# Ending the third and fourth spans of an opening's work order one row earlier

## The chip, the cores and the metric

One Trainium2 chip, one of its cores. The metric is the device time of one execution in microseconds (us), the median over runs of the same program. The engines are named as in the profile: PE is TensorE's matmul, PEld its weight load, DVE is VectorE, ACT is ScalarE, POOL is GpSimd, SP is SyncE, which here does nothing but issue DMAs.

## The reference

A trunk of two layers over 256 tokens of 2048 features. Each layer is a token mixer followed by a gated feed-forward network; ahead of each of these stands an RMS norm with a scale and a shift that are computed from a conditioning vector `c`. Layer 0 mixes with retention over 8 heads, layer 1 with a short convolution. The change lies in the beginning of layer 0:

```python
c_act = silu(c)
mod = c_act @ w_mod[i] + b_mod[i]                  # w_mod[i]: 2048 x 12288
sh1, sc1, g1, sh2, sc2, g2 = split(mod, 6)
h = rms_norm(x, norm1_g[i]) * (1 + sc1) + sh1      # 256 x 2048
q, k, v, g = split(h @ ret_w_in, ...)              # 2048 x (2048 + 2048 + 4096 + 4096)
q, k = rope(q), rope(k) * 256 ** -0.5              # 8 heads of 256
o = rms_norm(retention(q, k, v))                   # decaying causal attention, 8 heads
x = x + g1 * ((silu(g) * o) @ ret_w_out)
```

All arrays are float32.

## The kernel before, in words

Tokens lie in the free dimension. The 2048 features of `h` are 16 blocks of 128 partitions, called rows 0 to 15 (`h[k]`). A product of one row with one block of 128 output columns is a unit; its weights are a 128x128 block (64 KB). Each float32 operand is split in a high part (`hi`, rounded to the type fp32r) and a low rest (`lo`), and a product is three fast matmuls, hi*hi, hi*lo and lo*hi, into one PSUM bank half. The weights stand in memory in the order of use (`w_all`), cut into chunks of 128x2048, that is 16 units or 1 MB. A chunk is fetched by SP into one of four `raw` buffers, and `prepare` splits half of it (a piece, 8 units) at a time: a cast on ACT (line 426, `hi`), then a subtraction on DVE (line 429, `lo`). There are five places for split pieces, and two pieces are kept ready ahead of the one in use.

Before a row can be used, its scale and shift must be known, and these are products of `c` with 1 MB of `w_mod` each. The weights of row k are loaded by `loaded` (two DMAs), reduced on DVE against the activated `c` (`reduced`, line 805, one for SC1, one for SH1), turned into two columns on ACT (line 814), and applied to the normed `x` (ACT lines 832 and 833, DVE line 834, which writes the row's low part). Line 823 norms the `x` of two rows (`norm_two`). So every row costs 2 MB of DMA and two long DVE instructions, and while the rows come in one by one, PE is given products that need only the rows that exist. This opening is a written-out order in five spans, `SPANS`, each a pair of heads (or one) with a range of rows. All partial sums of a span, q (two column blocks), k (two) and g (four) of each head, are held open in PSUM: eight banks for a pair of heads, four for one head. Within a row the head's two q blocks go to its first bank, the two k blocks to its second, the 512 columns of g to its third and fourth, one for each half of the tokens; then comes the second head.

At the end of a span its banks are emptied by `held`: the first time for a head by an ACT copy to SBUF (line 792), the second time by a DVE addition to that copy (line 789). Of a span's eight additions, four are issued at once and four are put in the list of due work:

```python
for i, pt in enumerate(span(g, plain_rows if g is RET_SPANS[1] else ())):
    key = (heads[i // 4], i % 4)
    if key not in ahead or i < 4:
        held(key, pt)
    else:
        due.append((step[0] + 0.2 * (i - 4), lambda key=key, pt=pt: held(key, pt)))
```

The order on DVE and ACT is as issued here. `more` is called at the start and in the middle of each row of a span. It issues all work of the list `due` whose time has come, and then moves the clock `step` on; a row of a pair of heads is one step (16 units), a row of one head half a step. Row k is due (`row_due`) 1.4 steps after the one before for the first two, 1.8 for the next two, 2.2 for the others: row 8 at step 10.8, row 9 at 13.0, row 10 at 15.2, row 11 at 17.4, row 15 at 26.2. One third of the way to the next row stands the reduction SC1 of that next row, two thirds of the way `after_scale` with its reduction SH1 and, every other row, `norm_two`. If a span needs a row that hasn't been issued, `more` issues all of the list up to that row at once, whatever its time. `row_due` also asks SP for the `w_mod` of the row after next.

After the spans come the heads in the order 4, 0, 2, 1, 5, 3, 6, 7. For each, q, k and g are finished over the rows that the spans left out (`pair`; these are the usual products), v is computed over all rows, and scores and outputs follow. The q and k blocks of heads 1 and 3 go through `product` (lines 479 and 482: one matmul of 512 and one of 256 columns for a unit), all others through `packed` (three of 256 columns, lines 541 to 543, or for 512-wide weights three of 512 columns for each half of the tokens, lines 492 to 494). From the end of the spans, reductions of later modulations (line 333) are mixed in by `paced`, 28 of them between unit `early` and unit 1024, where `early` is the number of units in the spans.

Of the kernel before, what the change touches and what calls it, by code (L numbers as in the profile page):

```python
# [30 lines left out]

CHUNK = 2048
HALF = 1024
SPANS = (((0, 1), (0, 2)), ((2, 3), (0, 5)), ((0, 1), (2, 10)), ((2, 3), (5, 13)), ((4,), (0, 16)))
HEAD_ORDER = (4, 0, 2, 1, 5, 3, 6, 7)
ROW_STEPS, ROWS_AT, PREPARED = (1.4, 1.8, 2.2), (4, 6), 1.0
ON_SCALAR, ON_VECTOR, SUMMED = ((0, 1, -1, 2, 3, -2, 4, 6, -3, -4), ((0, 1), (2, 3), 5, (4, 5), 7, (6, 7)), (1, 3, 5, 7))
# [42 lines left out]
def ret_in_groups():  # L80

    qkg, v = [], []
    for h in range(HEADS):
        q = [Q0 + h * DK + i * P for i in range(2)]
        k = [K0 + h * DK + i * P for i in range(2)]
        qkg.append([q, k, [(G0 + h * DV, DV)]])
        v.append(Group([V0 + h * DV], DV))  # L90
    done = [0] * HEADS
    spans = []
    for heads, (a, b) in SPANS:
        assert all(done[h] == a for h in heads)
        for h in heads:
            done[h] = b
        spans.append(Group([c for h in heads for part in qkg[h] for c in part], ks=range(a, b)))
    rest = [[Group(c, ks=range(done[h], KT)) for c in qkg[h]] for h in range(HEADS)]
    return spans, list(zip(rest, v))
# [6 lines left out]
def out_groups(parts, tail, lead):  # L106

    cols = [c * P for c in range(KT)]
    out = []
    for ks in parts:  # L110
        led = cols[:lead]
        out.append([Group(led, ks=ks[:-tail])] + [Group([c], ks=ks[-tail:]) for c in led])
        out[-1] += [Group([c], ks=ks) for c in cols[lead:]]
    return out


def head_rows():

    n = DV // P
    ks = [n * h + i for h in HEAD_ORDER for i in range(n)]  # L120
    return [ks[: len(ks) // 2], ks[len(ks) // 2 :]]
# [6 lines left out]
RET_SPANS, RET_HEADS = ret_in_groups()  # L128
FIRST_KS = SPANS[0][1][1]
RET_OUT = out_groups(head_rows(), DV // P, LEAD_RET)  # L130
# [135 lines left out]
def trunk(ctx: ExitStack, tc: tile.TileContext, x_in, c_in, pos_in, w_mod, cols_in, gain_in, tab_in, w_all, out):  # L266
# [462 lines left out]
    with ExitStack() as inner:  # L729
# [64 lines left out]
        with tc.tile_pool(name="start", bufs=1) as sp:  # L794
# [196 lines left out]
            def span(g, plain=()):  # L991
                n = g.n // 2
                return packed(
                    g, h, before=lambda k: more(n, k), between=lambda k: more(n), banks=[bank() for _ in range(n)],
                    plain=plain,
                )

            with tc.manual_schedule(engines={mybir.EngineType.DVE, mybir.EngineType.Activation}):
                for (heads, _), g in zip(SPANS[1:-1], RET_SPANS[1:-1]):
                    for i, pt in enumerate(span(g, plain_rows if g is RET_SPANS[1] else ())):  # L1000
# [576 lines left out]
```

## Time and profile before

| | |
|---|---|
| median of 3 runs | 2555.41 us (2555.26 to 2556.01) |
| the profiled execution | 2555.34 us, of it 2553.6 us in the profile's span |
| PE busy | 2539.3 us (99%) |
| PEld busy | 2184.0 us (86%) |
| DVE busy | 2352.9 us (92%) |
| ACT busy | 1352.8 us (53%) |
| DMA | 689.49 MB, mean 270 GB/s |
| granted TensorE clock | 0.998 of full speed |

The page gives each engine's busy time; matmuls are pipelined, and the duration given for one is longer than the distance to the next, so the distance between starts is what a matmul costs in a stream. In a timeline a line has the start in us from the span's beginning, the duration, the engine, the line of the program, the operation with output<-input, a count of merged instructions, and, where the engine was idle before, for how long and what ended it. A table by windows has for each stretch its length, then the busy time and number of instructions (x) for PE, PEld, DVE, ACT and POOL, then the granted clock, the DMA engines' share and the GB/s moved.

### The profile page before, as it was taken

The page shows a single profiled execution, that of the slowest core. Times are in us where ns is not written, and L with a number is a line of the kernel's source. Part 1 is how long each engine was busy: PE and PEld are TensorE (multiplying, and loading weights), DVE is VectorE, ACT ScalarE, POOL GpSimd, SP SyncE. Part 2 cuts the span into 40 slices and gives each one's busy share as a digit, 9 for nine tenths or more (in the row PEclk, how much of TensorE's full clock was granted, in tenths as well). Part 3 has the DMA queues.
Part 4 walks back from the last instruction along what each step waited for, and adds up shares of the span by engine and source line. Part 5 has one row for each costly group of instructions (what it writes and reads, how often), then busy time and mean ns, then how long its engine had stood idle before and what let it go on. Part 6 is the DMA issues. An engine that isn't in the chain of part 4 may idle for free.

```text
span 2553.6 us, 34841 instructions
## 1 busy us (share of the span) xinstructions
PE 2539.3 (99%) x13281; PEld 2184.0 (86%) x13281; DVE 2352.9 (92%) x2967; ACT 1352.8 (53%) x1800; POOL 182.4 (7%) x234
## 2 busy tenths in 40 slices
PE   9999999999999999999999999999999999999998
PEld 7898888888889888888888898888998888888887
DVE  7989999898899999889999899888989999999998
ACT  5544543454456554345555454445566555555555
POOL 0000121011110001000000012000000000000001
PEclk9999999999999999999999999999999999999999
DMA  9977888879875667866568879888845565565653
GB/s 398 414 314 270 314 319 339 333 286 334 324 281 214 237 232 297 338 246 231 214 231 302 324 275 338 321 305 308 322 159 215 180 229 216 181 215 182 230 183 148
DMA packets 96698, 689.49 MB, mean 270 GB/s; under 512 B 10745, under 2 KB 12169, under 8 KB 13457
## 3 DMA queue, kind: packets, MB, share of 16 engines
q1 hardware_dynamic: 96528, 687.25, 72.3%
q8 instruction: 104, 1.70, 0.3%
q14 instruction: 66, 0.53, 0.1%
HBM read 685.11 MB, written 2.11 MB: 269 GB/s over the span
## 4 chain that ended last, share of the span: by engine, by line
PE 93%; DVE 4%; DMA 1%; issue 1%; ACT 0%; POOL 0%; ACTq 0%; POOLq 0%; SPq 0%; DVEq 0%
PE bank L479 22%; PE bank L492 17%; PE bank L493 17%; PE bank L494 17%; PE bank L482 11%; DVE lo L429 2%; PE bank L543 1%; PE bank L542 1%; PE bank L541 1%; PE bank L674 1%; PE bank L676 1%; PE bank L675 1%; PE bank L1304 1%; PE bank L1081 1%; DMA raw<-w_mod 1%; DMA raw<-w_all 1%
## 5 line engine op out<-in xcount | busy, mean ns | idle before, releaser
L426 ACT CAST hi<-raw 128x1024 fp32r<-128x1024 f32 (+1 forms) x984 | 992.0, 1019 | 952.6 <-PE bank L494 337.0
L429 DVE TENSOR_TENSOR lo<-raw,hi 128x1024 fp32r<-128x1024 f32 (+1 forms) x984 | 1142.3, 1178 | 123.7 <-ACT hi L426 113.5
L492 PE MATMUL bank<-hi,h 128*128 128x512 f32 x1540 | 602.2, 391 | 0.0
L493 PE MATMUL bank<-lo,h 128*128 128x512 f32 x1540 | 600.8, 390 | 0.0
L494 PE MATMUL bank<-hi,h 128*128 128x512 f32 x1540 | 600.1, 390 | 0.0
L333 DVE SCALAR_TENSOR_TENSOR raw<-raw,cb 128x2048 f32<-128x2048 f32 x160 | 365.5, 2286 | 9.2 <-DMA raw<-w_mod 8.9
L479 PE MATMUL bank<-h,hi 128*128 128x512 f32 x1012 | 352.7, 392 | 0.0
L494 PEld LDWEIGHTS bank<-hi,h 128*128 128x128 f32 x1540 | 289.3, 188 | 60.8
L492 PEld LDWEIGHTS bank<-hi,h 128*128 128x128 f32 x1540 | 289.4, 188 | 57.9
L493 PEld LDWEIGHTS bank<-lo,h 128*128 128x128 f32 x1540 | 289.5, 188 | 57.3 <-DVE lo L429 0.4
L479 PE MATMUL bank<-mid,hi 128*128 128x512 f32 x920 | 319.4, 391 | 0.0
L482 PE MATMUL bank<-h,lo 128*128 128x256 f32 x1012 | 284.8, 281 | 0.0
L482 PE MATMUL bank<-mid,lo 128*128 128x256 f32 x920 | 259.5, 282 | 0.0
L479 PEld LDWEIGHTS bank<-h,hi 128*128 128x128 f32 x1012 | 190.0, 188 | 40.4
L479 PEld LDWEIGHTS bank<-mid,hi 128*128 128x128 f32 x920 | 172.7, 188 | 35.8
L482 PEld LDWEIGHTS bank<-h,lo 128*128 128x128 f32 x1012 | 191.5, 189 | 0.5
L482 PEld LDWEIGHTS bank<-mid,lo 128*128 128x128 f32 x920 | 174.2, 189 | 0.1
L479 PE MATMUL bank<-rm,hi 128*128 128x512 f32 x496 | 172.5, 391 | 0.0
L482 PE MATMUL bank<-rm,lo 128*128 128x256 f32 x496 | 139.9, 282 | 0.0
L492 PE MATMUL bank<-hi,mid 128*128 128x512 f32 x284 | 110.7, 390 | 0.0
L494 PE MATMUL bank<-hi,mid 128*128 128x512 f32 x284 | 110.6, 389 | 0.0
L493 PE MATMUL bank<-lo,mid 128*128 128x512 f32 x284 | 110.6, 389 | 0.0
(301 smaller groups left out, 3352.7 us busy)
## 6 DMA issues: line engine op xcount, KB each, us to landing
raw<-w_all SPq DMA_DIRECT2D x456, 1024.0 KB, 4.9
raw<-w_mod SPq DMA_DIRECT2D x192, 1024.0 KB, 6.0
x<-x_in SPq DMA_DIRECT2D x4, 512.0 KB, 5.6
out<-xt SPq DMA_DIRECT2D x4, 512.0 KB, 2.7
decay<-tab_in SPq DMA_DIRECT2D x8, 128.0 KB, 5.4
x<-gate_row SPq DMA_DIRECT2D x2, 512.0 KB, 4.7
last_gain<-gain_in SPq DMA_DIRECT2D x1, 1024.0 KB
cols<-cols_in SPq DMA_DIRECT2D x1, 152.0 KB, 8.4
```

The source lines that it names most:

```text
L333: nc.vector.scalar_tensor_tensor(raw, raw, 1.0, cb, op0=ALU.mult, op1=ALU.mult, accum_out=total)
L426: nc.scalar.copy(hi[:, o], raw[:, o])
L429: nc.vector.tensor_tensor(lo, raw, hi.bitcast(F32), op=ALU.subtract)
L479: nc.tensor.matmul(pt, hi, h, start=fresh and k == g.ks[0], stop=False, skip_group_check=True)
L482: nc.tensor.matmul(pt[:, 1, :], lo, h[:, 0, :], start=False, stop=last and k == g.ks[-1], skip_group_check=True)
L492: nc.tensor.matmul(o, hi, w_hi, start=first, stop=False)
L493: nc.tensor.matmul(o, hi, w_lo, start=False, stop=False)
L494: nc.tensor.matmul(o, lo, w_hi, start=False, stop=last)
L541: nc.tensor.matmul(pt, hi, h[:, 0, :], start=first, stop=False, skip_group_check=True)
L542: nc.tensor.matmul(pt, hi, h[:, 1, :], start=False, stop=False, skip_group_check=True)
L543: nc.tensor.matmul(pt, lo, h[:, 0, :], start=False, stop=last, skip_group_check=True)
L674: nc.tensor.matmul(pt, hi, high, start=k == 0, stop=False, skip_group_check=True)
```

## The change

The third span (heads 0 and 1) ends with row 8 in place of row 9, and the fourth (heads 2 and 3) with row 11 in place of row 12. Row 9 of heads 0 and 1 and row 12 of heads 2 and 3, 16 units each, are computed with the heads' remaining rows after the opening. The layout of the weights follows, and so does `early`, which falls from 496 units to 464. Nothing else is edited.

```diff
-SPANS = (((0, 1), (0, 2)), ((2, 3), (0, 5)), ((0, 1), (2, 10)), ((2, 3), (5, 13)), ((4,), (0, 16)))
+SPANS = (((0, 1), (0, 2)), ((2, 3), (0, 5)), ((0, 1), (2, 9)), ((2, 3), (5, 12)), ((4,), (0, 16)))
```

## The prediction

> **What bounds the kernel now.** I read the page's first lines first, then its chain that ended last, then the list of what PE waited for.
>
> ```profile
> span 2553.6 us, 34841 instructions
> PE 2539.3 (99%) x13281; PEld 2184.0 (86%) x13281; DVE 2352.9 (92%) x2967; ACT 1352.8 (53%) x1800; POOL 182.4 (7%) x234
> PE 93%; DVE 4%; DMA 1%; issue 1%; ACT 0%; POOL 0%; ACTq 0%; POOLq 0%; SPq 0%; DVEq 0%
> PE bank L543 <- DVE lo L429: 1.8, 3, 0.9
> PE bank L542 <- DVE h L834: 0.3, 1, 0.3
> PE bank L1081 <- DVE sp L559: 0.5, 1, 0.5
> ```
>
> PE carries the end: 93% of the chain is its own. The last three lines are waits of PE in the first 250 us (us in total, times, longest); the first of them lies ahead of the changed place and is touched by nothing here. From 108 us to the end of the span the list has one entry, the 0.5 us on `sp`. So every us by which PE stalls in the opening is a us of the total, and there is hardly a wait left behind the opening that could be won back.
>
> The opening itself has two other engines near their limit, as the table by windows shows.
>
> ```profile
> 4.00:8.00 4.00, 2.77 (x12) 1.91 (x12) 0.77 (x3) 2.71 (x6) 0.00 (x0) 0.92 0.97 373
> 8.00:12.00 4.00, 4.00 (x15) 3.34 (x15) 3.27 (x5) 2.62 (x5) 0.00 (x0) 0.66 1.04 424
> 64.00:68.00 4.00, 3.13 (x20) 2.67 (x19) 4.00 (x6) 3.72 (x9) 0.00 (x0) 1.00 1.01 422
> 96.00:120.00 24.00, 23.71 (x150) 21.19 (x149) 23.54 (x28) 10.64 (x14) 0.00 (x0) 1.00 1.01 420
> 168.00:192.00 24.00, 24.00 (x158) 21.95 (x157) 18.38 (x19) 12.43 (x17) 0.00 (x0) 1.00 0.73 272
> ```
>
> From 96 to 120 us DVE is busy 23.54 of 24 us and the DMA engines all of the time; by 168 us both have slack. The changed boundary falls in the tight stretch. PE's timeline there:
>
> ```profile
> 99.61 0.28 PE L541 MATMUL bank<-h,hi 128*128 128x256 f32 x1
> 101.04 0.40 PE L492 MATMUL bank<-hi,h 128*128 128x512 f32 x1
> 101.74 0.40 PE L492 MATMUL bank<-hi,h 128*128 128x512 f32 x1
> 102.20 0.39 PE L494 MATMUL bank<-hi,h 128*128 128x512 f32 x1
> 102.43 0.28 PE L541 MATMUL bank<-h,hi 128*128 128x256 f32 x1
> 105.25 0.31 PE L541 MATMUL bank<-h,hi 128*128 128x256 f32 x1
> 105.85 0.39 PE L542 MATMUL bank<-h,hi 128*128 128x256 f32 x1 [0.29 <-DVE h L834]
> 108.66 0.28 PE L541 MATMUL bank<-h,hi 128*128 128x256 f32 x1
> 111.47 0.28 PE L541 MATMUL bank<-h,hi 128*128 128x256 f32 x1
> ```
>
> Row 8 of the third span runs from 99.61 to 105.25 us, one head from 99.61 to 102.43. Half a row costs 2.82 us, a row 5.64. Within the half, the g matmuls begin 1.43 us after its start (101.04), those for the second half of the tokens 0.70 later (101.74). Row 9 starts at 105.25, and its first half takes 108.66 - 105.25 = 3.41 us in place of 2.82: PE loses 0.59 us for the low part of row 9, forced at step 12 ahead of its due time 13.0.
>
> **The change part by part.** First, the row that PE waits for. The third span no longer uses row 9; its first use moves to the fourth span, step 16, three steps behind its due time. Gone: **-0.59 us**. Late next is not another row but what takes its place, the emptying of the banks. Both spans need all eight, so the fourth span's first row can't write a bank before the third's sum has been added from it (`held`). Before, this came after the rush for row 9, and DVE did it so:
>
> ```profile
> 97.50 0.42 DVE L834 TENSOR_TENSOR h<-u,h 128x256 fp32r<-128x256 f32 x1
> 99.21 2.28 DVE L805 SCALAR_TENSOR_TENSOR raw<-raw,cb 128x2048 f32<-128x2048 f32 x1
> 101.42 2.29 DVE L805 SCALAR_TENSOR_TENSOR raw<-raw,cb 128x2048 f32<-128x2048 f32 x1
> 103.64 0.69 DVE L823 TENSOR_TENSOR two<-x,rb 128x512 f32<-128x512 f32 x1
> 104.24 1.22 DVE L429 TENSOR_TENSOR lo<-raw,hi 128x1024 fp32r<-128x1024 f32 x1
> 105.38 0.42 DVE L834 TENSOR_TENSOR h<-u,h 128x256 fp32r<-128x256 f32 x1
> 107.25 3.07 DVE L789 TENSOR_TENSOR rm<-rm,bank 128x512 f32<-128x512 f32 x5
> 110.23 1.22 DVE L429 TENSOR_TENSOR lo<-raw,hi 128x1024 fp32r<-128x1024 f32 x1
> 111.37 1.28 DVE L789 TENSOR_TENSOR rm<-rm,bank 128x512 f32<-128x512 f32 x2
> 113.70 0.68 DVE L789 TENSOR_TENSOR rm<-rm,bank 128x512 f32<-128x512 f32 x1
> 114.30 2.29 DVE L805 SCALAR_TENSOR_TENSOR raw<-raw,cb 128x2048 f32<-128x2048 f32 x1
> ```
>
> One sees row 8's low part (97.50), the two reductions for row 9 and a norm (99.21 to 104.24), row 9's low part (105.38), and then eight additions as 5, 2 and 1 among splits, with no reduction until 114.30. The seventh ended by 112.6, and its bank, the second head's first g bank, was wanted at 114.3 + 1.43 = 115.7: hidden, by 3 us. From start to start, an addition costs (110.23 - 107.25)/5 = 0.60 us, a split 111.37 - 110.23 = 1.14, a reduction 101.42 - 99.21 = 2.21, the norm 104.24 - 103.64 = 0.60.
>
> After, the span's end is at step 12, while the reductions of row 9 keep their times, 11.53 (SC1) and 12.27 (SH1, with the norm); `more` issues only at whole and half steps, so they come out at 12.0 and 12.5. The deferred additions are due at 12.0, 12.2, 12.4 and 12.6. Sorted, the order on DVE becomes: additions 0 to 3, SC1, addition 4, split, addition 5, SH1, norm, addition 6, split, addition 7, split, row 9's low part. Two reductions and the norm now stand among the additions. Up to 99.21 us both programs are the same. The fourth addition waits for its bank's last matmul, 102.20 + 0.39 = 102.59. From there: addition to 103.19, SC1 to 105.40, addition 4 to 106.00, split 107.14, addition 5 to 107.74, SH1 109.95, norm 110.55, addition 6 ends 0.68 after that start, 111.23; the split begins at 111.15 and gives way at 112.29, addition 7 ends at 112.97.
>
> PE starts the fourth span at 105.25 and wants the second head's first g bank at 105.25 + 2.82 + 1.43 = 109.50. It gets it at 111.23: 1.73 us lost. The second bank is wanted 0.70 later, at 111.93, and is free at 112.97: 1.04 more. **+2.77 us**. The banks of both heads' q and k and of the first head's g are free in time (addition 5 at 107.74 against 108.07 + 0.71). The split weights for the next row are ready by 112.29. Bounds for this term: nothing at the low end, as before, where the same additions hid; at the high end 2.77 plus one more reduction ahead of addition 7, 2.21, so 4.98. I take the worked value, since every duration in it is a row.
>
> Queued behind these on DVE: the split for the row after next (wanted near 119) and row 9's low part, now near 114.4 us, wanted at step 16, past 128 us. SP is held up too: `w_mod` of row 11, two issues behind row 9, and a chunk of `w_all` wait until those `raw` buffers are read, near 110 to 112 us. They are used 12 us and more later, so I cost them nothing; DMA will show a gap instead.
>
> The second boundary, span four to five, comes at step 19 with the reductions of row 12 at the same places, but the fifth span takes four banks, and the four immediate additions free these: nothing. The fifth span starts two steps sooner, so rows 13 to 15 are wanted 11.3 us earlier against their due times. Row 15 is the tight one:
>
> ```profile
> 184.79 0.28 PE L541 MATMUL bank<-h,hi 128*128 128x256 f32 x1
> 184.80 0.42 DVE L834 TENSOR_TENSOR h<-u,h 128x256 fp32r<-128x256 f32 x1 [0.31 <-ACT h L833]
> 187.62 0.28 PE L541 MATMUL bank<-h,hi 128*128 128x256 f32 x1
> ```
>
> It is issued in the middle of the row that starts at step 26, and its low part ended at 185.22, 0.43 us after that row's start (184.79). After, the very next row, 2.83 us on, is row 15: a margin of 2.4 us, where DVE is busy 18.38 of 24. Nothing.
>
> The moved units: 32 in all, of which the q and k units of heads 1 and 3, 2 x 4, change from three 256-column matmuls to one of 512 and one of 256.
>
> ```profile
> 306.31 0.39 PE L479 MATMUL bank<-h,hi 128*128 128x512 f32 x1
> 306.66 0.40 PE L479 MATMUL bank<-h,hi 128*128 128x512 f32 x1
> ```
>
> Such a unit takes 306.66 - 306.31 = 0.35 us; in the opening four take 1.43, so 0.357. Eight units: -0.06 us. The other 24 run the same matmuls. Their weight splits (four pieces, 4.6 us of DVE) and two `w_all` chunks of 1 MB move with them, behind PE. `paced` keeps its 28 reductions, each with its DMA and its small POOL operations, over 560 units in place of 528: thinner, no cost. With them moves the 0.5 us wait on `sp`: it may go, or double.
>
> Sum: 2555.34 - 0.59 + 2.77 - 0.06 = 2557.46. The profiled execution stands 0.07 under the median of 2555.41, so I forecast 2557.5 us, 0.08% slower. A measurement here tells about 0.2%, 5.1 us, from no change; this is inside it.
>
> **The rivals.** *The additions stay hidden* and only the wait for row 9 goes: 2555.41 - 0.65 = 2554.8. It needs additions 6 and 7 ahead of SH1, or a DVE that runs 3.5 us earlier. For it: before, all eight hid. Against: DVE's order follows the list, and DVE has no slack there.
>
> *PE's clock falls in the stall.* In the windows, 4 to 8 us has PE busy 2.77 of 4 us and the clock at 0.92, then 0.66: a loss of (0.08 + 0.34) x 4 = 1.7 us. 64 to 68 has 3.13 busy at 1.00. The predicted stall leaves PE busy some 2.3 us in one stretch of 4, nearer to the first. That gives 2557.5 + 1.7 = 2559.2. [...]
>
> *Slower by over 0.2%: row 15 comes late.* Place: the last row of the fifth span. It decides once its low part comes more than 2.4 us later against PE than before; from there each us is a us. To pass 2560.5 takes 2.4 + 3.0 = 5.4 us. For it: 11 us of lead are given up. Against: DVE's slack there, and the same work at the same steps. At 6 us late the time is 2561.1.
>
> *Faster by over 0.2%* has no place: PE's waits from the boundary on are 0.59 and 0.5.
>
> **How the numbers follow.** Forecast 0.60; additions hidden 0.20; clock 0.12; row 15 late, or another stall of that size, 0.06; faster 0.02. The range goes from the hidden case less 0.2 of scatter, 2554.6, to the clock case with the `sp` wait doubled and some of the upper bound, 2560.0. The forecast's own range is 2556.9 to 2558.3. Within 0.2% lie the first three, 0.92.
>
> **What would show it.** In the changed trace PE has no wait for `h` at 105 us, but two waits on DVE's line 789 in the first row of the fourth span, near 111 and 113 us, of about 1.7 and 1.0 us, and line 805 stands between additions. The clock stays at 1.00. The DMA share dips after 105 us. No wait is seen at row 15. It is wrong if PE waits on something else there, if line 789 shows no wait, or if the heads' part grows.

## The result, and the profile after

The changed kernel takes 2564.67 us (median of 5 runs, 2563.68 to 2566.73) against 2555.66 us before: ratio 1.0036, interval 1.0025 to 1.0046, 9.0 us slower. The span of its profiled execution is 9.2 us longer. The page's first lines, the one group of PE on the page that now has idle time before it, and PE's waits from 80 to 250 us (total, times, longest; behind 250 us there are none):

```profile
span 2562.8 us, 34842 instructions
PE 2543.1 (99%) x13273; PEld 2185.2 (85%) x13273; DVE 2356.0 (92%) x2967; ACT 1354.7 (53%) x1800; POOL 182.5 (7%) x234
L492 PE MATMUL bank<-hi,h 128*128 128x512 f32 x1540 | 601.8, 391 | 2.4 <-DVE rm L789 2.4
PE bank L1054 <- ACT k L1025: 2.4, 1, 2.4
PE bank L492 <- DVE rm L789: 2.4, 2, 1.7
PE bank L1081 <- ACT sp L558: 1.4, 1, 1.4
PE bank L1057 <- DVE k L1026: 0.6, 1, 0.6
```

The work is the same; the waits are not. Two are the forecast ones on the additions (line 789). The others are for `k` and `sp` of head 4, the first head behind the opening. PE's timeline gives what each place costs:

```profile
108.47 0.28 PE L541 MATMUL bank<-h,hi 128*128 128x256 f32 x1
114.26 0.28 PE L541 MATMUL bank<-h,hi 128*128 128x256 f32 x1
190.41 0.28 PE L541 MATMUL bank<-h,hi 128*128 128x256 f32 x1
217.57 0.57 PE L1054 MATMUL bank<-q,k 128*128 128x512 f32 x1 [2.43 <-ACT k L1025]
226.81 0.96 PE L1081 MATMUL bank<-v,sp 128*128 128x512 f32 x3 [1.38 <-ACT sp L558]
231.84 0.28 PE L541 MATMUL bank<-h,hi 128*128 128x256 f32 x1
```

The fourth span's first row: its second half takes 114.26 - 108.47 = 5.79 us in place of 2.82, **+2.97**; row 9's 0.59 is saved. Row 15 starts at 190.41, and the matmuls behind head 4's second output group at 231.84: 41.43 us. Before, the same two points were at 198.90 and 233.54:

```profile
198.90 0.28 PE L541 MATMUL bank<-h,hi 128*128 128x256 f32 x1
233.54 0.28 PE L541 MATMUL bank<-h,hi 128*128 128x256 f32 x1
```

That is 34.64 us, so **+6.79**. The sum, 2.97 - 0.59 + 6.79 = 9.17, accounts for the 9.2 us (this execution came to the place 0.4 us later than the one before, and about as much is made up behind head 4). Of the 6.79, 2.4 and 0.6 are waits for k (its high part, then its low part) and 1.4 one for sp, less the 0.5 us on sp that was there before. Nearly all of the rest, 2.9 us, is in the clock. By windows (length, busy time and count of PE, PEld, DVE, ACT, POOL, then granted clock, DMA share, GB/s):

```profile
216.00:217.00 1.00, 0.00 (x0) 0.00 (x0) 1.00 (x4) 0.81 (x2) 0.00 (x0) 1.00 0.90 377
218.00:219.00 1.00, 0.42 (x2) 0.28 (x2) 1.00 (x3) 0.00 (x0) 0.00 (x0) 0.50 0.90 377
222.00:223.00 1.00, 1.00 (x7) 1.00 (x6) 1.00 (x3) 0.00 (x0) 0.00 (x0) 0.50 0.00 0
224.00:225.00 1.00, 1.00 (x7) 1.00 (x7) 1.00 (x1) 0.00 (x0) 0.00 (x0) 0.65 0.76 131
```

After the wait PE ran at half its clock from about 218 to 224.7 us, from 218.72 on through matmuls without a gap.

### The profile page after: what moved, and what is told of

Its sections match the earlier page's. It is cut to its first block, busy times and chain, and to the rows that moved or that the text cites. A ratio compares the mean times of both kernels' runs of the same rounds, so it can differ in the third digit from the quotient of the medians.

```text
span 2562.8 us, 34842 instructions
## 1 busy us (share of the span) xinstructions
PE 2543.1 (99%) x13273; PEld 2185.2 (85%) x13273; DVE 2356.0 (92%) x2967; ACT 1354.7 (53%) x1800; POOL 182.5 (7%) x234
## 4 chain that ended last, share of the span: by engine, by line
PE 94%; DVE 3%; DMA 1%; issue 1%; ACT 0%; POOL 0%; ACTq 0%; POOLq 0%; DVEq 0%; SPq 0%
PE bank L479 22%; PE bank L492 17%; PE bank L493 17%; PE bank L494 17%; PE bank L482 11%; DVE lo L429 1%; PE bank L543 1%; PE bank L541 1%; PE bank L542 1%; PE bank L674 1%; PE bank L676 1%; PE bank L675 1%; DMA raw<-w_all 1%; PE bank L1304 1%; PE bank L1081 1%
```

## The experiments

Each is an edit of the changed kernel, unless it says otherwise; differences are between medians of runs on the same chip.

**held_at_once**

```diff
-                        if key not in ahead or i < 4:
+                        if True:
```

> The changed kernel with all eight additions of a span issued at its end, none deferred, so that no reduction stands between them. What the changed trace has to be explained: the boundary costs 2.97 us there (half a row that takes 5.79 us in place of 2.82), head 4's scores and what follows cost another 6.8 us, and 0.59 us is saved on row 9; sum 9.2 us. Theory 'two places': the boundary and the scores are separate, so this run loses the 2.97 us and keeps the rest, about +6.2 us on the kernel before; the order on DVE after the opening is the same as in the changed kernel, so the wait for k at head 4's scores stays about 2.4 us. Rival 'one place': the stall at the boundary shifts DVE and PE against each other and causes the late k; then both go, and the time is 0.6 us under the kernel before. [...]

Measured: 2561.84 us, +5.9 on the kernel before (ratio 1.0023, 1.0013 to 1.0032). PE's wait on line 789 is gone, and the waits at head 4 are there to the tenth:

```profile
PE bank L1054 <- ACT k L1025: 2.4, 1, 2.4
PE bank L1081 <- ACT sp L558: 1.4, 1, 1.4
```

So there are two places, and the first costs what its row says.

**angles_early**

```diff
-                due.append((at + (i + 1) * 0.5, turn))
+                due.append((at - 5.0 + (i + 1) * 0.5, turn))
```

> The changed kernel with the six steps of the rope's angles due 5 steps sooner, within the fifth span, so that they no longer stand behind row 15's low part. Theory 'chain': k of head 4 is late (2.4 us wait, then 0.6 for its low part, then a clock of 0.50 for 7 us, then 1.4 on sp) because angles, rope of q and rope of k start only when row 15 is done, and in the changed kernel row 15 is done half a row before the spans' end. Then these waits go and what is left is the boundary: -0.59 + 2.97, and less the 0.5 us wait on sp that the kernel before had: +1.9 to +2.4 us on the kernel before, no clock under 1.00 after 200 us. Rival 'reductions': the reductions of later modulations, which begin 32 units sooner, push k; then the wait shrinks little and the time stays near +9 us. Rival 'row 15': row 15 itself is late; then the angles put ahead of it make it later, and the time grows.

Measured: 2566.89 us, +11.0 (1.0028 to 1.0058). The wait for k is gone, and a longer one stands elsewhere:

```profile
PE bank L542 <- DVE h L834: 5.1, 1, 5.1
189.88 0.41 ACT L833 CAST h<-u 128x256 fp32r<-128x256 f32 x1
194.40 1.22 DVE L429 TENSOR_TENSOR lo<-raw,hi 128x1024 fp32r<-128x1024 f32 x1 [1.38 <-ACT hi L426]
198.02 0.42 DVE L834 TENSOR_TENSOR h<-u,h 128x256 fp32r<-128x256 f32 x1
```

ACT had row 15's high part ready at 190.3. DVE reached its low part at 198.02, behind the angles and behind splits that themselves waited for casts. That is the third rival of this run, and it is the prediction's rival of a late row 15, here by another cause. Row 15 in the changed kernel itself was in time. The 11 us are not the late row's alone: in this profile the clock fell too, at the boundary (0.50 from 114 to 118 us) and behind the long wait (0.53 and 0.62 in the windows of 198 to 202 us).

**warm_wait**

```diff
                 pt = bank()
+                for _ in range(10 if head == 4 and jt == 0 else 0):
+                    nc.tensor.matmul(pt[:, 0, :P], ones, ones, start=True, stop=True, skip_group_check=True)
```

> The changed kernel with ten matmuls of 128x128 ones put ahead of head 4's first score, into the bank that the scores then overwrite. They have nothing to wait for, so they fill the 2.4 us in which PE stands idle for k, and cost nothing as long as k is that late. Theory 'clock': the idle PE makes the granted clock fall to 0.50 for 6.8 us, in which 256-column matmuls take 0.213 us in place of 0.119, worth some 3 us; with PE kept busy the clock stays at 1.00, and the time is about +6 us on the kernel before. Rival 'late k alone': the clock costs nothing, because the next wait, on sp, takes up what it would save; then +9 us as in the changed kernel. [...]

Measured: 2564.56 us, +8.6 (1.0021 to 1.0044), no different from the changed kernel. The clock did stay at 1.00, but the wait that followed took most of it up. The edit moved the lines behind it, so that 1083 is the old 1081; 579 is what it was:

```profile
218.00:220.00 2.00, 1.35 (x10) 1.22 (x10) 1.90 (x4) 0.45 (x2) 0.00 (x0) 1.00 0.92 385
222.00:224.00 2.00, 0.81 (x7) 0.61 (x6) 2.00 (x5) 1.21 (x2) 0.31 (x1) 1.00 0.27 33
PE bank L1083 <- ACT sp L558: 1.4, 1, 1.4
PE bank L1083 <- DVE sp L559: 0.8, 1, 0.8
PE bank L579 <- ACT acc L565: 1.6, 1, 1.6
```

PE ran through the matmuls at its full clock and stood waiting for sp, whose low part DVE began only 1.6 us sooner (225.21 in place of 226.79). PE was 1.6 us ahead behind head 4, and in this execution lost it far behind the opening, at 1856 us, to a wait (the last line) that the changed kernel's profile doesn't have. The profiled execution took 2564.62 us, and three of the seven were near 2562.8, so that wait may not stand in all of them. So about half of what the clock cost hid inside DVE's lateness: the limit at this place is DVE, and the rival was nearer than the theory.

**plan_as_before**

```diff
-    plan_mod = [(early, 0), (1024, 28), (1984, 72), ...
+    plan_mod = [(early + 32, 0), (1024, 28), (1984, 72), ...
```

> The changed kernel with the plan of the later modulations' reductions put back: it starts 32 units behind the spans' end, at unit 496, as before. Theory 'reductions': these reductions, 2.2 us of DVE each, stand ahead of k because the plan starts sooner; with them later k is in time and the time is +2.4 us on the kernel before. Theory 'chain' (the angles start too late against the spans' end): in the changed kernel as in the one before two reductions stand ahead of k, so their number is not what changed; but one fewer would win back 2.2 us, about all of the 2.4 us wait. So if the order on DVE now has one reduction fewer ahead of k, both theories give +2.4 to +3.5 us, and the run only prices a reduction; if the wait stays, +9 us, and the reductions are not it.

Measured: 2558.55 us, +2.6 (1.0001 to 1.0019). From 60 to 260 us PE's longest waits are the two on the additions (2.4 us together, as in the changed kernel), and the only other one is 0.7 us on a `lo`. All of head 4's 6.8 us is gone, with the opening untouched. DVE's timelines show how, in rows picked out of them, first the changed kernel, then this one:

```profile
191.69 1.23 DVE L429 TENSOR_TENSOR lo<-raw,hi 128x1024 fp32r<-128x1024 f32 x1 [1.39 <-ACT hi L426]
199.56 2.28 DVE L333 SCALAR_TENSOR_TENSOR raw<-raw,cb 128x2048 f32<-128x2048 f32 x1
208.04 2.28 DVE L333 SCALAR_TENSOR_TENSOR raw<-raw,cb 128x2048 f32<-128x2048 f32 x1
216.78 1.29 DVE L1041 TENSOR_TENSOR v<-bank,v 128x512 fp32r<-128x512 f32 x2
217.98 0.69 DVE L1026 TENSOR_TENSOR k<-qa,k 128x512 fp32r<-128x512 f32 x1
220.72 2.28 DVE L333 SCALAR_TENSOR_TENSOR raw<-raw,cb 128x2048 f32<-128x2048 f32 x1
223.47 2.28 DVE L333 SCALAR_TENSOR_TENSOR raw<-raw,cb 128x2048 f32<-128x2048 f32 x1
226.79 0.42 DVE L559 TENSOR_TENSOR sp<-sum,sp 128x256 fp32r<-128x256 f32 x1 [1.02 <-ACT sp L558]
```

```profile
207.63 2.29 DVE L333 SCALAR_TENSOR_TENSOR raw<-raw,cb 128x2048 f32<-128x2048 f32 x1
214.16 0.69 DVE L1026 TENSOR_TENSOR k<-qa,k 128x512 fp32r<-128x512 f32 x1
215.91 1.28 DVE L1041 TENSOR_TENSOR v<-bank,v 128x512 fp32r<-128x512 f32 x2
219.30 0.62 DVE L559 TENSOR_TENSOR sp<-sum,sp 128x256 fp32r<-128x256 f32 x2
```

In the changed kernel two reductions (line 333) and v's split stand ahead of k, and two more among the score sums ahead of sp. With the plan put back, one stands ahead of k, none among the sums, and v comes behind k: k 3.8 us sooner, sp 7.5. As the expectation says, one reduction fewer fits both of its theories, so the run shows that room on DVE is enough, and not that the reductions are what had been added.

**third_alone**: the fourth span is left at row 12.

```diff
-SPANS = (..., ((0, 1), (2, 9)), ((2, 3), (5, 12)), ((4,), (0, 16)))
+SPANS = (..., ((0, 1), (2, 9)), ((2, 3), (5, 13)), ((4,), (0, 16)))
```

> Half of the change: the third span ends with row 8, the fourth still with row 12. Behind the opening one step is lost against row 15 in place of two. Theory 'boundary plus lead': the boundary costs its 2.97 us less the 0.59 us of row 9 in full, +2.4 us, and head 4's scores cost something between nothing and a third of the 6.8 us, since the splits and reductions stand there only in part as in the changed kernel: +2.4 to +4.5 us in all. Rival 'the two halves add': each half costs half of the 9 us, +4.5 us here and +4.5 us for the fourth span alone.

Measured: 2560.97 us, +5.1 (1.0009 to 1.0028): over the first theory's range. Head 4 has one wait of 1.6 us on sp. The rest is at the boundary, where in this execution the clock fell too:

```profile
114.00:116.00 2.00, 2.00 (x10) 1.85 (x10) 2.00 (x4) 1.05 (x1) 0.00 (x0) 0.53 0.75 295
116.00:118.00 2.00, 2.00 (x10) 1.82 (x10) 2.00 (x2) 0.00 (x0) 0.00 (x0) 0.61 1.02 426
```

That cost some 1.5 us on top of the 2.97; I had not put it in the expectation.

**fourth_alone**: the third span is left at row 9.

```diff
-SPANS = (..., ((0, 1), (2, 9)), ((2, 3), (5, 12)), ((4,), (0, 16)))
+SPANS = (..., ((0, 1), (2, 10)), ((2, 3), (5, 12)), ((4,), (0, 16)))
```

> The other half: the fourth span ends with row 11, the third still with row 9. No additions meet reductions at the third span's end, so the 2.97 us are not there, and the 0.59 us wait for row 9 is still there. Theory 'boundary plus lead': 0 to +2 us, all of it at head 4's scores, where PE's wait for k is under 1 us and the clock stays at 1.00. Rival 'the two halves add': +4.5 us.

Measured: 2557.28 us, +1.4 (0.9997 to 1.0016), within the first theory. PE waits 1.4 us on sp, not on k. The halves give 5.1 + 1.4 = 6.5 us, the whole 9.0, and 1.5 of the 5.1 were the clock at the boundary. At head 4 alone, from its first score to the first matmul behind its second output group, the traces have 10.06 us before (223.48 to 233.54), 11.24 with the third span alone (222.16 to 233.40) and 11.01 with the fourth alone (218.64 to 229.65): +1.2 and +1.0 us, against +6.8 for both. The costs of lateness at head 4 do not add.

**angles_at_20**

```diff
-                due.append((at + (i + 1) * 0.5, turn))
+                due.append((at - 9.0 + (i + 1) * 0.5, turn))
```

> The changed kernel with the angles due 9 steps sooner in place of 5, from step 19.9 on, so that they are done before the reductions for row 15 and can't hold up its low part, as they did with 5 steps (PE waited 5.1 us for it there). Theory 'chain': DVE has all of the rope's inputs when q and k are done, k is in time, no wait at head 4's scores, and the wait on sp is gone too; what is left is the boundary less row 9 and less the 0.5 us on sp that the kernel before had: +1.4 to +2.4 us. Rival 'reductions': the later modulations' reductions still start at the spans' end and still keep k or sp waiting, over 1 us each; then +4 us or more.

Measured: 2560.68 us, +4.8 (1.0008 to 1.0027). No wait at head 4, on k or on sp, although the plan stood as in the changed kernel: the chain theory holds on that. The time missed its range, because the angles held up splits where they now stood, and the clock fell at the boundary in this profile as well (0.50 from 114 to 116 us). Of the 1.3 us below, 0.7 is the old wait at 66 us; 0.27 and 0.28 at 179 and 182 us are new.

```profile
PE bank L543 <- DVE lo L429: 1.3, 3, 0.7
PE bank L542 <- DVE h L834: 0.5, 1, 0.5
```

**angles_at_20_held_at_once**: both edits, `if True:` and `at - 9.0`.

> The same with all eight additions issued at a span's end. With both costs taken away the change is left with what it was to give: row 9's 0.59 us, 0.06 us of cheaper units and the 0.5 us wait on sp: 1.0 to 1.2 us under the kernel before, 2554.6 us or so. If something else of the change costs time, a wait that stood behind these two, it shows here: then the time is over that of the kernel before.

Measured: 2557.14 us, +1.3 (0.9994 to 1.0013). The gain of 1.0 to 1.2 us that was forecast did not come. What PE waits for are late splits from 171 to 178 us (0.41, 0.27 and 0.27 us) and a late row at 190 (0.50 us): the price of the angles' new place, not of the spans.

**held_at_once_plan_as_before**: both edits, `if True:` and `early + 32`.

> The changed kernel with all eight additions issued at a span's end and the plan of the later reductions at unit 496 as before: the two edits that took away one cost each, together. Each cost was seen to go with no new wait in its place. Theory 'two places': what is left is row 9's 0.59 us, 0.06 us of cheaper units and the wait on sp of 0.3 to 0.5 us: 0.9 to 1.1 us under the kernel before, 2554.8 us, and little scatter, since no stall of PE is long enough for the clock to fall. Rival: a cost of the change that is in neither place; then the time is at or over that of the kernel before.

Measured, 11 runs: 2554.71 us, 1.2 us under the kernel before, ratio 0.9993 (0.9984 to 1.0002). Behind 60 us PE has the old wait on `lo`, 0.7 us, and far behind the opening two of 0.2 us. The forecast of this run was right in size, but the interval takes in 1: not shown to be faster.

**before_plan_later**: the kernel before, with `early + 32` in the plan.

> The control for it: the kernel before, its spans unchanged, with the plan of the later reductions 32 units later (at unit 528). If the gain of the kernel with both edits comes from the spans, this one wins only the 0.3 to 0.5 us of the wait on sp. If it is the plan alone that gains, both gain alike, and the change of the spans is worth nothing.

Measured, 11 runs: 2556.93 us, +1.0 (0.9994 to 1.0011). The waits on sp did not go, so a later plan by itself gains nothing. The 1.2 us of the run above, as far as it is real, is not the plan's.

**rows_sooner_held_at_once**

```diff
-ROW_STEPS, ROWS_AT, PREPARED = (1.4, 1.8, 2.2), (4, 6), 1.0
+ROW_STEPS, ROWS_AT, PREPARED = (1.4, 1.8, 2.0), (4, 6), 1.0
```

(with `if True:` as well)

> The changed kernel with all eight additions at once, and with rows 7 to 15 due every 2.0 steps in place of 2.2, which puts row 15 two steps sooner: against the spans' end it is as early as in the kernel before, and four halves of v's weights are split ahead of the angles again, as there. The later reductions stand on DVE as in the changed kernel: two ahead of k, two among the scores' sums ahead of sp. This tells what of the 6.8 us at head 4's scores is due to DVE's waits for casts among the angles (2.3 us there) and what to the reductions. Theory 'lead': with the lead back the wait for k goes, and at most the 1.4 us on sp stays: -0.6 to +1.0 us. Theory 'reductions': they stand where they stood, so k and sp are as late as before and the time is that of the changed kernel with the additions at once, about +6 us. Against both: rows that come faster ask more of DVE and DMA from 90 us on, and a row or a weight may be late there.

Measured: 2561.51 us, +5.6 (1.0012 to 1.0030), the size that the theory 'reductions' gave. Row 15's low part came at 174.25 us, 13 us ahead of the changed kernel's, and head 4 waits as before:

```profile
PE bank L1054 <- ACT k L1025: 2.2, 1, 2.2
PE bank L1081 <- ACT sp L558: 1.4, 1, 1.4
```

So the lead of row 15 isn't what was lost. Whether DVE's waits for casts play a part it can't say, since splits that waited stood among the angles here too.

## Why the prediction was wrong

**The boundary: right.** The order on DVE, the two waits and their places came as worked out: 1.67 and 0.76 us on line 789, at 111.7 and 113.5, where I had 1.73 and 1.04. The cost in time is 2.97 us against 2.77; row 9's wait went. Rows of DVE, picked out:

```profile
100.92 2.80 DVE L789 TENSOR_TENSOR rm<-rm,bank 128x512 f32<-128x512 f32 x4 [1.22 <-PE bank L543]
103.63 2.28 DVE L805 SCALAR_TENSOR_TENSOR raw<-raw,cb 128x2048 f32<-128x2048 f32 x1
108.17 2.29 DVE L805 SCALAR_TENSOR_TENSOR raw<-raw,cb 128x2048 f32<-128x2048 f32 x1
110.98 0.68 DVE L789 TENSOR_TENSOR rm<-rm,bank 128x512 f32<-128x512 f32 x1
112.72 0.68 DVE L789 TENSOR_TENSOR rm<-rm,bank 128x512 f32<-128x512 f32 x1
```

PE's first use of the banks and every start here lie 0.4 us behind my table, which is how much later this execution reached the place. The DMA gap is there as well: 94 GB/s from 112 to 114 us. The second boundary costs nothing, and row 15's margin was right:

```profile
187.59 0.43 DVE L834 TENSOR_TENSOR h<-u,h 128x256 fp32r<-128x256 f32 x1 [0.32 <-ACT h L833]
```

It ends 2.4 us ahead of its use at 190.41, the figure of the prediction.

**The step that failed** is the last of the moved parts: "`paced` keeps its 28 reductions ... thinner, no cost. With them moves the 0.5 us wait on `sp`: it may go, or double." I counted the reductions by units and never laid out DVE's queue between row 15 and head 4's scores, as I had done for the boundary. It was a full queue (before, DVE was busy for 23.96 of the 24 us from 206 to 230; the slack that I had read from 168 to 192 was over), and the 0.5 us wait on sp was its sign. Head 4 cost 6.79 us there, where I had 0 to 0.5. That the plan's start moved with `early` is a part of the cause without which it isn't there: putting the start back at its old unit takes the 6.8 us away. It is not the only such part, since taking the angles out of the queue removed the waits too. The common cause is the length of DVE's queue ahead of k and sp.

The reductions were not more, as far as k goes. Two stand ahead of it in the kernel before as well; ahead of sp it is three before and four after. From the first of the angles (line 750) to the last operation that k's high part needs (line 1023), first before, then after:

```profile
195.68 0.29 DVE L750 CAST angles<-angles 128x256 f32<-128x256 int32 x1
204.70 2.29 DVE L333 SCALAR_TENSOR_TENSOR raw<-raw,cb 128x2048 f32<-128x2048 f32 x1
213.05 2.29 DVE L333 SCALAR_TENSOR_TENSOR raw<-raw,cb 128x2048 f32<-128x2048 f32 x1
219.66 0.41 DVE L1023 TENSOR_TENSOR qa<-qa,bank 128x256 f32<-128x256 f32 x1
```

```profile
187.93 0.29 DVE L750 CAST angles<-angles 128x256 f32<-128x256 int32 x1
216.45 0.42 DVE L1023 TENSOR_TENSOR qa<-qa,bank 128x256 f32<-128x256 f32 x1
```

That is 28.52 us in place of 23.98. The 4.54 more are two splits (ten in place of eight, 1.14 us each) and 2.26 us in which DVE waited for casts (0.26, 1.39 and 0.61; before, none). So the plan put back took a reduction out of a queue that other work had made longer.

What turned DVE's order stays open. Behind the opening that order isn't written out by hand but chosen by the framework's scheduler, and against the spans' end the reductions are asked for at almost the same units in both kernels (every 19 and every 20). No run takes DVE's waits for casts among the angles away by themselves; in plan_as_before they stand as in the changed kernel, and k is in time.

**The clock** was named as a rival, at the boundary, for 1.7 us, chance 0.12. Six profiles have the boundary's stall. In three the clock stayed at 1.00 there (the changed kernel, warm_wait, plan_as_before); in three it fell, for about 1.5 us in those of the third span alone and of the angles at step 20 and for about 2.8 us in that of angles_early. So the fall is measured in half of them, its size was near the rival's, and the chance was too low. That the sum has nothing for it was my estimate, which no run had shown: the longest wait of PE in the kernel before is 1.2 us. One step of the rival's working is wrong: it has PE busy for 2.3 of 4 us, but its own two stalls both lie between 109.50 and 112.97, which leaves 4 - 1.73 - 1.04 = 1.2. In the changed kernel's profile the clock fell at head 4, a place that I had not looked at. There it cost little by itself: with the clock kept up, PE was 1.6 us further.

## What to carry to other kernels

When a stage ends sooner, what is tied to its end (the emptying of its banks, any plan that counts from there) moves against what is tied to a clock of its own; write out the queue of the second engine at every place where the two meet, not only at the place that is edited. Here a wait of half a us on an engine that is otherwise hidden marked a queue without slack: price the change at such a place first. Take such costs away one at a time and together, since here the costs of lateness at one place did not add up.

## What the runs showed of the hardware

The clock fell to half behind stalls of PE of 2.4 us and less. At head 4 of the changed kernel PE stood for 2.43 us, and the clock was 0.50 from 218 to 224 us. At the boundary PE stood for 1.67 and 0.77 us with 1.0 us of matmuls between, and in the run with the third span alone the clock was 0.53 and 0.61 in the next two windows of 2 us (114 to 118 us). The same stall, 1.67 and 0.76 us, left the clock at 1.00 in the profile of the changed kernel (110 to 120 us). What decides between the two, no run shows. The wait of 0.87 us on `lo`, ahead of 65.91 us in the kernel before, left it at 1.00 (64 to 68 us).

At head 4 the half clock lasted 6.8 us, some 6 of them with PE busy without a gap. In the changed kernel's windows of 1 us from 216 to 226 us the clock was 1.00 or 0.50, but for the two in which it changed (0.93 from 217, 0.65 from 224 us). Taken as whole or half everywhere, a window of 2 us with granted clock c holds 4 x (1 - c) us at half clock. Summed so, the falls at the boundary and at head 4 came in two lengths. They are 3.4 us with the third span alone, in angles_at_20 (0.86, 0.50 and 0.79 from 112 to 118 us) and held_at_once (0.58 and 0.57 from 216 to 220 us), as in rows_sooner_held_at_once (256-column matmuls 0.21 us apart from 216.8 to 220.2 us, and 0.12 behind that), and 6.8 us in the changed kernel and in angles_early (0.69, 0.50, 0.50 and 0.60 from 112 to 120 us).
